# Appending each batch's new keys to its cached-key tile, a one-pass bias and a transposed head pick in a decoder step's sampled-token attention

## Chip, core and metric

The program runs on one core of one Trainium2 chip. The metric is the device time of one launch in microseconds (us). Before the change the median of three runs is 1094.81 us (1094.43 to 1094.97).

## What is computed

One inference step of a two-layer decoder on 288 tokens: 256 prompt tokens and 8 batches of 4 sampled tokens. Each layer projects the tokens, runs four mixers side by side (pooling, Conformer convolution, short convolution, sparse attention), merges them by gates, and applies a SwiGLU channel mixer and two layer norms. The part that matters here is the sampled tokens' attention: every sampled token looks at its batch's 256 cached positions (two pages of 128, found by a page table) and at its batch's up to 4 new positions, keeps the 65 best by an indexer's score, and attends to those with 8 heads of 64:

```python
ki_all = jnp.concatenate([cache_kidx.reshape(-1, IDX_DIM)[row_ids].astype(ki.dtype), ki], axis=1)
sc = index_scores(qi, ki_all, wi)
sc = jnp.where(jnp.arange(past + t)[None, None, :] <= qpos[None, :, None], sc, -jnp.inf)
vals, idx = lax.top_k(sc, ktop)
...
return sparse_attend(q, kg, vg, jnp.isfinite(vals))
```

## The kernel before

Activations stand feature by token, [128, 8, 288]. All projections go through `mm3` (L268): each float32 weight tile and each activation is split into a high and a low part of type fp32r, and three products (L271 to L273) are summed. Weights come in groups of 8 tiles (512 KB); the whole program has 306 groups, as 2448 tiles. `W` (L256) starts a turn with each group g: it issues the load of group g+5 on the SP queue, the high part of group g+3 on ACT (L245, `whi`) and the low part of group g+2 on DVE (L252, `wlo`, three buffers), and then calls `side` (L200).

`side` is the planner. Mixers and attention are generators ("tasks"). Each turn has a budget of 1.96 us of DVE and 2.3 us of ACT; the ready tasks are stepped in the order in which they were started, round after round, until one of the two budgets is used up. A task yields a pair (DVE cost, ACT cost) after what it emitted, or a number of turns to sleep, so that another engine's result is there before it goes on. All that a step emits, TensorE work too, is put on the engines' queues at that place: after the turn's `wlo` on DVE, and ahead of the group's 24 matmuls on TensorE. Tasks marked low (the convolution, 62 multiply-adds of L643 and L645 a layer) run when nothing else is ready. `finish` runs a task to its end where its result is needed.

The tasks that the change touches are two. `index_sample` (L879) loads the indexer's cached keys into one `kv` tile (16 transfers), spreads the queries into `qibd` (L886), takes scores against cached keys (L892) and, in a second bank, against all 32 new keys (L894, masked later by `vb`), sums the heads by `ws` (L902, L907), runs the top-65 on [32, 288] and leaves 0 or -1e30 per position in `sbias` (L914). `attn_sample` (L918) works on two halves f of four batches. Per half, in order:

- `load_pages("ck", f)`: eight transfers of 256 KB, each 128 partitions of 2 KB, into four `kv` tiles.
- Logits in one PSUM bank of 288 columns: the bias of each row by a float32 product with the selector `selh` (L936), four products with all new keys into columns 256 to 287 (L939), and 16 products with the cached keys, 32 rows each (L943).
- Row maximum (L948, L950 on DVE), `load_pages("cv", f)`, exponent on ACT (L954), a turn's sleep, reciprocal on DVE (L958), three transposes on TensorE (L962, L963), copies on ACT (L965, L966), a turn's sleep.
- Values: L971 for the new ones, L974 for the cached ones. Each of the 128 rows (batch, head, token) then holds 512 columns of which its own head's 64 count: DVE multiplies by the reciprocal and a head mask (L978), and TensorE picks the rows of each token with the 0/1 matrix `sel16` (L987, four float32 products of 16 columns). ACT and DVE split the result into high and low part (L992, L995).

Of the kernel before, what the change touches and what calls it, by code (L numbers as in the profile page):

```python
# [10 lines left out]
F32 = mybir.dt.float32  # L11
# [26 lines left out]
BIG = -1.0e30  # L38
# [12 lines left out]
def constants():  # L51
# [15 lines left out]
    ok = (b_[:, None] == b_[None, :]) & (t_[None, :] <= t_[:, None])  # L67
    vb = np.zeros((128, NS))
    vb[:NS] = np.where(ok, 0.0, NEG)
# [11 lines left out]
    c["selh"] = sh.reshape(128, 256)  # L81
    c["hmask"] = (h[:, None] == (np.arange(H))[None, :]) * 1.0
    c["sel16"] = ((j * TS + t)[:, None] == np.arange(16)[None, :]) * 1.0
# [10 lines left out]
    return [np.concatenate(p, 1).astype(np.float32) for p in parts], off  # L94


CONST, COFF = constants()
# [14 lines left out]
class Builder:  # L112
# [3 lines left out]
    def __init__(self, tc, ctx, d):  # L116
# [15 lines left out]
        self.hold = False  # while set, a new group's turn emits loads alone  # L132

# [97 lines left out]
    def fetch(self, g, only=0):  # L231
        """Loads, first and second parts of the groups up to so far ahead of g, or one of the three alone."""
# [74 lines left out]
    # The deviations are taken from the mean of the first half of the features, p, as soon as that is known:  # L307
    # with m the mean of d = r - p, which is at most the standard deviation, var = mean(d^2) - m^2.
    def ln_part(self, k):
        """r's chunk k is in xf (from the second half on: d's)"""  # L310
        nc, xf = self.nc, self.xf
        if k == 0:
            self.lnt = self.b([128, 4, N])
        elif k == 1:
            nc.gpsimd.tensor_tensor(self.lnt[:, 0], xf[:, 0], xf[:, 1], op=OP.add)  # L315
        elif k < 4:
            nc.gpsimd.tensor_tensor(self.lnt[:, 0], self.lnt[:, 0], xf[:, k], op=OP.add)  # L317
        else:
            self.sqs.append(k)
# [6 lines left out]
    def ln_pivot(self, scale=None):  # L326
        """xf less p, its second half scaled before"""
# [32 lines left out]
    def ln(self, g, b, after=None, fill={}):  # L360
        """fill: functions for some places that emit matrix products, and return one that takes the results away."""
# [490 lines left out]
    def load_kidx(self):  # L852
        nc, l, d = self.nc, self.l, self.d
        self.kx = self.sb.tile([128, 4, 2, 128], F32, name="kv", tag="kv", bufs=4)
        rows = slice(PHYS * l, PHYS * (l + 1))
        for b in range(NB):
            for g in range(2):
# [3 lines left out]
                nc.sync.dma_start(self.kx[64 * (b % 2):64 * (b % 2) + 64, b // 2, g],  # L861
# [4 lines left out]
    def load_pages(self, which, f):  # L866
# [3 lines left out]
        for b in range(4 * f, 4 * f + 4):  # L870
            t = self.sb.tile([128, 2, 4, 128], F32, name="kv", tag="kv", bufs=4)
            for g in range(2):
                nc.sync.dma_start(t[:, g].rearrange("p c k -> p (c k)"),
                                  d[which][rows][ds(self.page[2 * b + g], 1)].rearrange("a p k -> p (a k)"))
            out.append(t)
# [3 lines left out]
    def index_sample(self):  # L879
# [4 lines left out]
        for r in range(2):  # L884
            for h in range(4):
                nc.scalar.activation(self.qibd[64 * r:64 * r + 64, :, r, h],  # L886
                                     qv[64 * (h % 2):64 * (h % 2) + 64, h // 2, :, r], AF.Copy)
                yield 0, 0.22
        yield 1
        a, a2 = yield from self.get_ax(2)  # L890
        for p in range(4):
            nc.tensor.matmul(a[32 * p:32 * p + 32, :TP], self.qibd[:, p].rearrange("p r h t -> p (r h t)"),  # L892
                             self.kx[:, p].rearrange("p g k -> p (g k)"), start=True, stop=True)
        nc.tensor.matmul(a2[:, :NS], self.qibd.rearrange("p g r h t -> p (g r h t)"), self.ki[:, TP:],  # L894
                         start=True, stop=True)
        nc.tensor.matmul(a2[:, 64:64 + NS], self.c("hsel")[:4], self.wi[:, TP:], start=True, stop=True)
        rl = self.sb.tile([128, N], F32, name="rls", tag="rls", bufs=1)
        nc.scalar.activation(rl[:, :TP], a[:, :TP], AF.Relu, scale=0.0625)
        nc.scalar.activation(rl[:, TP:], a2[:, :NS], AF.Relu, scale=0.0625)
        yield 0, 0.6  # L900
        ws = self.sb.tile([128, NS], F32, name="ws", tag="ws", bufs=1)
        nc.vector.tensor_tensor(ws, a2[:, 64:64 + NS], self.c("delta"), op=OP.mult)  # L902
        self.free_ax(2)
# [3 lines left out]
        nc.tensor.matmul(a[:NS, :N], ws, rl, start=True, stop=True)  # L907
        sc = self.sb.tile([NS, N], F32, name="scs", tag="scs", bufs=1)
        nc.scalar.activation(sc[:, :TP], a[:NS, :TP], AF.Copy)
        nc.vector.tensor_tensor(sc[:, TP:], a[:NS, TP:N], self.c("vb")[:NS], op=OP.add)  # L910
        self.free_ax()
        yield 0.2, 0.3
        yield from self.topk(sc, NS, N, TOP_S)
        nc.vector.tensor_scalar(sc, sc, MARK, BIG, op0=OP.not_equal, op1=OP.mult)  # L914
        yield 0.3, 0
        self.sbias = sc

    def attn_sample(self):  # L918
# [12 lines left out]
        for f in range(2):  # L931
            if f:
# [3 lines left out]
            nc.tensor.matmul(a[:, :N], self.c("selh")[:NS, 128 * f:128 * (f + 1)], self.sbias,  # L936
                             start=True, stop=False)
            for c in range(4):
                nc.tensor.matmul(a[:, TP:N], self.qbd[:, c, 4 * f:4 * f + 4].rearrange("p b h t -> p (b h t)"),  # L939
                                 self.k[:, c, TP:], start=False, stop=False)  # L940
            for c in range(4):
                for j in range(4):
                    nc.tensor.matmul(a[32 * j:32 * j + 32, :TP],  # L943
                                     self.qbd[:, c, 4 * f + j].rearrange("p h t -> p (h t)"),
                                     kt[j][:, :, c], start=False, stop=c == 3)
            yield 1
            st = self.sb.tile([128, 3], F32, name="sts", tag="sts", bufs=2)
            nc.vector.tensor_reduce(st[:, 0:1], a[:, :N], axis=AX.X, op=OP.max)  # L948
# [4 lines left out]
            p = self.sb.tile([128, N], F32, name="rls", tag="rls", bufs=1)  # L953
            nc.scalar.activation(p, a[:, :N], AF.Exp, scale=0.125, bias=st[:, 0:1], accum_out=st[:, 1:2])  # L954
            self.free_ax()
            yield 0, 0.5
            yield 1
            nc.vector.reciprocal(st[:, 2:3], st[:, 1:2])  # L958
            yield 0.1, 0
# [3 lines left out]
            nc.tensor.transpose(a[:NS, 256:384], p[:, TP:], ident)  # L963
# [8 lines left out]
            for kc in range(2):  # L972
                for j in range(4):
                    nc.tensor.matmul(a[32 * j:32 * j + 32], pt[:, kc, 32 * j:32 * j + 32],  # L974
                                     vc[j][:, kc].rearrange("p c k -> p (c k)"),
                                     start=False, stop=kc == 1)
            m = yield from self.get_b([128, 512])
            nc.vector.scalar_tensor_tensor(m.rearrange("p (h d) -> p h d", h=H),  # L978
                                           a.rearrange("p (h d) -> p h d", h=H), st[:, 2:3],
                                           self.c("hmask")[:, :, None].to_broadcast([128, H, DH]),  # L980
                                           op0=OP.mult, op1=OP.mult)
            self.free_ax()
            yield 0.65, 0
            yield 1
            a = yield from self.get_ax()
            for c in range(4):
                nc.tensor.matmul(a[:, 16 * c:16 * c + 16], m[:, 128 * c:128 * (c + 1)], self.c("sel16"),  # L987
                                 start=True, stop=True)
            self.free()
            w = slice(TP + 16 * f, TP + 16 * f + 16)  # L990
            v = a[:, :64].rearrange("p (c t) -> p c t", c=4)
            nc.scalar.activation(dp[0][:, :, w], v, AF.Copy)  # L992
            yield 0, 0.25
            yield 1
            nc.vector.tensor_tensor(dp[1][:, :, w], v, dp[0][:, :, w].bitcast(F32), op=OP.subtract)  # L995
            self.free_ax()
            yield 0.15, 0
# [365 lines left out]
```

## Time and profile before

| | |
|---|---|
| median of three runs | 1094.81 us |
| profiled execution, first to last instruction | 1094.1 us |
| TensorE matmul busy | 1066.6 us (97%), 8138 instructions |
| DVE busy | 768.2 us (70%) |
| ACT busy | 557.1 us (51%) |
| GpSimd (POOL) busy | 172.0 us (16%) |
| mean granted TensorE clock | 0.995 |
| DMA | 190.24 MB, 174 GB/s on average |

The profiled execution's own time is given by its span alone, 1094.1 us; the 0.7 us between it and the median lie outside the first and last instruction or are spread between executions. TensorE's queue is in order, and so are DVE's, ACT's and SP's: an instruction that waits holds up all behind it on its engine. A float32 product is shown as two matmul instructions (x2 for one product), an fp32r product and a transpose as one. Matmuls are pipelined: a matmul's duration (0.29 us for a product of the weight stream) is longer than the distance from its start to the next one's start (0.13 us), and it is the distance that counts for TensorE's time.

### The profile page before, as it was taken

How to read it: one execution, taken by the hardware profiler on the slowest of the kernel's cores; microseconds unless marked ns; L12 is line 12 of the kernel's file. 1: busy time of each engine (PE TensorE's matmuls, PEld its weight loads, DVE VectorE, ACT ScalarE, POOL GpSimd, SP SyncE). 2: the span in 40 equal slices, each digit the busy share in tenths (PEclk: the TensorE clock that was granted, in tenths of full speed). 3: DMA queues.
4: the chain of work that ended last, by engine and by line, in shares of the span. 5: the costliest groups of instructions: out<-in, count | busy, mean ns of one | idle time of the engine just before them, and what ended most of it. 6: DMA issues, size and time to landing. Idle time of an engine off the chain costs nothing.

```text
span 1094.1 us, 20642 instructions
## 1 busy us (share of the span) xinstructions
PE 1066.6 (97%) x8138; PEld 1029.7 (94%) x8138; DVE 768.2 (70%) x1302; ACT 557.1 (51%) x928; POOL 172.0 (16%) x169
## 2 busy tenths in 40 slices
PE   8899999999999999999998999999999999999996
PEld 7889989999999999999998899899999999999995
DVE  5897868866886555544779968786587855555456
ACT  4765555454564444333576654455645644443334
POOL 0640001104410000000416300030055000000004
PEclk9999999999999999999999999999999999999998
DMA  8467557344444544554354665465443554454431
GB/s 285 158 202 266 169 206 244 130 155 166 150 159 163 173 166 156 176 171 165 137 180 144 228 242 192 143 220 191 167 160 117 183 174 164 158 174 168 171 139 44
DMA packets 60531, 190.24 MB, mean 174 GB/s; under 512 B 7026, under 2 KB 10130, under 8 KB 60434
## 3 DMA queue, kind: packets, MB, share of 16 engines
q1 hardware_dynamic: 59442, 185.35, 49.4%
q0 software_dynamic: 992, 3.57, 0.9%
q8 instruction: 64, 1.05, 0.4%
q14 instruction: 33, 0.27, 0.1%
HBM read 184.15 MB, written 4.75 MB: 173 GB/s over the span
## 4 chain that ended last, share of the span: by engine, by line
PE 84%; DVE 10%; issue 2%; POOL 2%; DMA 2%; ACT 1%; SPq 0%; DVEq 0%; POOLq 0%
PE mm L271 23%; PE mm L272 23%; PE mm L273 23%; DVE wlo L252 3%; DVE b L645 3%; PE mm L295 2%; PE mm L293 2%; PE mm L297 2%; DMA wraw<-in_w_dram 1%; PE ax L272 1%; PE ax L273 1%; PE ax L271 1%; POOL b L317 1%; POOL b L348 1%; PE ax L943 1%
## 5 line engine op out<-in xcount | busy, mean ns | idle before, releaser
L252 DVE TENSOR_TENSOR wlo<-wraw,whi 128x1024 fp32r<-128x1024 f32 (+1 forms) x307 | 382.6, 1248 | 155.6 <-issue 73.1
L273 PE MATMUL mm<-xh,wlo 128*128 128x288 f32 x1536 | 454.3, 296 | 10.8 <-DVE wlo L252 10.8
L271 PE MATMUL mm<-xh,whi 128*128 128x288 f32 x1536 | 456.3, 297 | 0.0
L272 PE MATMUL mm<-xl,whi 128*128 128x288 f32 x1536 | 453.8, 295 | 0.0
L245 ACT ACTIVATE whi<-wraw 128x1024 fp32r<-128x1024 f32 (+1 forms) x307 | 322.4, 1052 | 157.6 <-PE mm L272 80.4
L273 PEld LDWEIGHTS mm<-xh,wlo 128*128 128x128 f32 x1536 | 289.0, 188 | 13.8 <-DVE wlo L252 13.8
L271 PEld LDWEIGHTS mm<-xh,whi 128*128 128x128 f32 x1536 | 289.5, 188 | 7.8 <-issue 6.0
L272 PEld LDWEIGHTS mm<-xl,whi 128*128 128x128 f32 x1536 | 289.3, 188 | 0.4
L271 PE MATMUL mm<-b,whi 128*128 128x288 f32 x576 | 170.8, 296 | 0.4 <-DVE m L1017 0.4
L272 PE MATMUL mm<-b,whi 128*128 128x288 f32 x576 | 170.2, 295 | 0.0
L273 PE MATMUL mm<-b,wlo 128*128 128x288 f32 x576 | 169.9, 295 | 0.0
L271 PEld LDWEIGHTS mm<-b,whi 128*128 128x128 f32 x576 | 108.5, 188 | 1.3 <-DVE m L1017 0.6
L272 PEld LDWEIGHTS mm<-b,whi 128*128 128x128 f32 x576 | 108.5, 188 | 0.3
L273 PEld LDWEIGHTS mm<-b,wlo 128*128 128x128 f32 x576 | 108.4, 188 | 0.0
L1021 POOL TENSOR_TENSOR m<-m,s 128x288 f32<-128x288 f32 x32 | 36.3, 1159 | 269.1 <-DVE s L1020 269.1
L315 POOL TENSOR_TENSOR b<-xf 128x288 f32<-128x288 f32 x4 | 4.9, 1215 | 442.0 <-DVE xf L1167 433.4
L1140 ACT ACTIVATE b<-s 128x288 fp32r<-128x288 f32 x44 | 19.3, 445 | 92.1 <-DVE s L1135 92.1
L645 DVE SCALAR_TENSOR_TENSOR b<-b,prm 128x256 f32<-128x256 f32 x120 | 65.3, 600 | 0.0
L1135 DVE TENSOR_TENSOR s<-s,mm 128x288 f32<-128x288 f32 x40 | 18.0, 454 | 50.3 <-PE mm L273 50.3
L1005 ACT ACTIVATE xf<-mm 128x288 f32<-128x288 f32 x32 | 13.1, 410 | 59.3 <-PE mm L273 59.2
L1005 ACT ACTIVATE g<-mm 128x288 f32<-128x288 f32 x32 | 13.1, 410 | 58.7 <-PE mm L273 58.7
L1143 DVE TENSOR_TENSOR b<-s,b 128x288 fp32r<-128x288 f32 x44 | 19.8, 458 | 19.4 <-ACT b L1140 19.4
(252 smaller groups left out, 1230.3 us busy)
## 6 DMA issues: line engine op xcount, KB each, us to landing
wraw<-in_w_dram SPq DMA_DIRECT2D x305, 512.0 KB, 3.5
kv<-in_ck_dram SPq DMA_DIRECT2D x32, 256.0 KB, 6.0
kv<-in_cv_dram SPq DMA_DIRECT2D x32, 256.0 KB, 4.8
out_ko_dram<-b POOLq DMA_DIRECT2D x2, 576.0 KB, 4.3
out_vo_dram<-b POOLq DMA_DIRECT2D x2, 576.0 KB, 7.1
b<-in_conv_ext_dram SPq DMA_DIRECT2D x2, 558.0 KB, 5.7
kv<-in_kidx_dram SPq DMA_DIRECT2D x32, 32.0 KB, 2.8
xf<-in_x_dram SPq DMA_DIRECT2D x3, 288.0 KB, 6.6
```

The costliest lines, as they stand in the source:

```text
L245: nc.scalar.activation(t[:, c], self.raw[self.nhi][:, c], AF.Copy)
L252: nc.vector.tensor_tensor(t[:, c], raw[:, c], self.hi[self.nlo][:, c].bitcast(F32), op=OP.subtract)
L271: m(out, wh, rh, start=first, stop=False)
L272: m(out, wh, rl, start=False, stop=False)
L273: m(out, wl, rh, start=False, stop=last)
L293: m(o, wh, rh[:, k], start=k == 0, stop=False)
L295: m(o, wl, rh[:, k], start=False, stop=False)
L297: m(o, wh, rl[:, k], start=False, stop=k == nk - 1)
L645: nc.vector.scalar_tensor_tensor(o, e, wj, o, op0=OP.mult, op1=OP.add)
L1005: self.nc.scalar.activation(g, a, AF.Sigmoid)
L1021: nc.gpsimd.tensor_tensor(self.m[:, j], self.m[:, j], t, op=OP.add)
L1143: nc.vector.tensor_tensor(h[:, 1, i % 2], t, h[:, 0, i % 2].bitcast(F32), op=OP.subtract)
```

## The change

The three new or changed ideas: the four new keys of a batch are copied behind its 256 cached keys, so that one product covers 260 columns, both for the indexer and for the logits; the bias is a single fp32r product (the selector and 0 or -2^100 are exact in that type); and instead of masking heads and picking rows by products, the normalised rows are transposed, and ACT and DVE read, per 64 partitions, the columns of the right head. The new values' probabilities, now 4 columns, are spread to 32 by a DVE product with the 0/1 constant `own` before they are transposed. `selh` is loaded on its own and rounded on GpSimd; `const1` loses 292 columns.

```diff
 MARK = -3.3e38
-BIG = -1.0e30
+BIG = -(2.0 ** 100)
+NK = TP + TS
 G = 8
...
     b_, t_ = bt // TS, bt % TS
-    ok = (b_[:, None] == b_[None, :]) & (t_[None, :] <= t_[:, None])
-    vb = np.zeros((128, NS))
-    vb[:NS] = np.where(ok, 0.0, NEG)
+    vb = np.zeros((128, TS))
+    vb[:NS] = np.where(np.arange(TS)[None, :] <= t_[:, None], 0.0, NEG)
     c["vb"] = vb
...
         sh[:NS, f] = bt[:, None] == ((4 * f + j) * TS + t)[None, :]
-    c["selh"] = sh.reshape(128, 256)
-    c["hmask"] = (h[:, None] == (np.arange(H))[None, :]) * 1.0
-    c["sel16"] = ((j * TS + t)[:, None] == np.arange(16)[None, :]) * 1.0
+    selh = sh.reshape(128, 256)[:NS].astype(np.float32)
+    c["own"] = np.concatenate([((4 * f + j)[:, None] == np.arange(NB)[None, :]) * 1.0 for f in range(2)], 1)
     win = np.array([2, 4, 8, 16])
...
         nc, l, d = self.nc, self.l, self.d
-        self.kx = self.sb.tile([128, 4, 2, 128], F32, name="kv", tag="kv", bufs=4)
+        self.kx = self.sb.tile([128, 4, NK], F32, name="kv", tag="kv", bufs=4)
         rows = slice(PHYS * l, PHYS * (l + 1))
...
                     self.page[i] = nc.sync.value_load(self.pt[0:1, i:i + 1], min_val=0, max_val=PHYS - 1)
-                nc.sync.dma_start(self.kx[64 * (b % 2):64 * (b % 2) + 64, b // 2, g],
+                nc.sync.dma_start(self.kx[64 * (b % 2):64 * (b % 2) + 64, b // 2, 128 * g:128 * (g + 1)],
                                   d["kidx"][rows][ds(self.page[2 * b + g], 1)].rearrange("a p k -> p (a k)"))
...
         for b in range(4 * f, 4 * f + 4):
-            t = self.sb.tile([128, 2, 4, 128], F32, name="kv", tag="kv", bufs=4)
+            own = which == "ck"
+            t = self.sb.tile([128, 4, NK] if own else [128, 2, 512], F32, name="kv", tag="kv", bufs=4)
             for g in range(2):
-                nc.sync.dma_start(t[:, g].rearrange("p c k -> p (c k)"),
-                                  d[which][rows][ds(self.page[2 * b + g], 1)].rearrange("a p k -> p (a k)"))
+                page = d[which][rows][ds(self.page[2 * b + g], 1)]
+                if own:
+                    nc.sync.dma_start(t[:, :, 128 * g:128 * (g + 1)], page.rearrange("a p (c k) -> p (a c) k", c=4))
+                else:
+                    nc.sync.dma_start(t[:, g], page.rearrange("a p k -> p (a k)"))
+            if own:
+                nc.scalar.activation(t[:, :, TP:], self.k[:, :, TP + TS * b:TP + TS * (b + 1)], AF.Copy)
+                yield 0, 0.22
             out.append(t)
...
                 yield 0, 0.22
+        kn = self.ki[:, TP:].rearrange("p (g r t) -> p g r t", g=4, r=2)
+        for r in range(2):
+            nc.scalar.activation(self.kx[64 * r:64 * r + 64, :, TP:], kn[64 * r:64 * r + 64, :, r], AF.Copy)
+            yield 0, 0.22
         yield 1
-        a, a2 = yield from self.get_ax(2)
+        a = yield from self.get_ax()
         for p in range(4):
-            nc.tensor.matmul(a[32 * p:32 * p + 32, :TP], self.qibd[:, p].rearrange("p r h t -> p (r h t)"),
-                             self.kx[:, p].rearrange("p g k -> p (g k)"), start=True, stop=True)
-        nc.tensor.matmul(a2[:, :NS], self.qibd.rearrange("p g r h t -> p (g r h t)"), self.ki[:, TP:],
-                         start=True, stop=True)
-        nc.tensor.matmul(a2[:, 64:64 + NS], self.c("hsel")[:4], self.wi[:, TP:], start=True, stop=True)
-        rl = self.sb.tile([128, N], F32, name="rls", tag="rls", bufs=1)
-        nc.scalar.activation(rl[:, :TP], a[:, :TP], AF.Relu, scale=0.0625)
-        nc.scalar.activation(rl[:, TP:], a2[:, :NS], AF.Relu, scale=0.0625)
-        yield 0, 0.6
+            nc.tensor.matmul(a[32 * p:32 * p + 32, :NK], self.qibd[:, p].rearrange("p r h t -> p (r h t)"),
+                             self.kx[:, p], start=True, stop=True)
+        nc.tensor.matmul(a[:, 288:288 + NS], self.c("hsel")[:4], self.wi[:, TP:], start=True, stop=True)
+        rl = self.sb.tile([128, NK], F32, name="rls", tag="rls", bufs=1)
+        nc.scalar.activation(rl, a[:, :NK], AF.Relu, scale=0.0625)
+        yield 0, 0.4
         ws = self.sb.tile([128, NS], F32, name="ws", tag="ws", bufs=1)
-        nc.vector.tensor_tensor(ws, a2[:, 64:64 + NS], self.c("delta"), op=OP.mult)
-        self.free_ax(2)
+        nc.vector.tensor_tensor(ws, a[:, 288:288 + NS], self.c("delta"), op=OP.mult)
+        self.free_ax()
         yield 0.1, 0
...
         a = yield from self.get_ax()
-        nc.tensor.matmul(a[:NS, :N], ws, rl, start=True, stop=True)
-        sc = self.sb.tile([NS, N], F32, name="scs", tag="scs", bufs=1)
+        nc.tensor.matmul(a[:NS, :NK], ws, rl, start=True, stop=True)
+        sc = self.sb.tile([NS, NK], F32, name="scs", tag="scs", bufs=1)
         nc.scalar.activation(sc[:, :TP], a[:NS, :TP], AF.Copy)
-        nc.vector.tensor_tensor(sc[:, TP:], a[:NS, TP:N], self.c("vb")[:NS], op=OP.add)
+        nc.vector.tensor_tensor(sc[:, TP:], a[:NS, TP:NK], self.c("vb")[:NS], op=OP.add)
         self.free_ax()
         yield 0.2, 0.3
-        yield from self.topk(sc, NS, N, TOP_S)
-        nc.vector.tensor_scalar(sc, sc, MARK, BIG, op0=OP.not_equal, op1=OP.mult)
+        yield from self.topk(sc, NS, NK, TOP_S)
+        sbias = self.sb.tile([NS, NK], F32R, name="wi", tag="wi", bufs=1)
+        nc.vector.tensor_scalar(sbias, sc, MARK, BIG, op0=OP.not_equal, op1=OP.mult)
         yield 0.3, 0
-        self.sbias = sc
+        self.sbias = sbias
...
             a = yield from self.get_ax()
-            nc.tensor.matmul(a[:, :N], self.c("selh")[:NS, 128 * f:128 * (f + 1)], self.sbias,
-                             start=True, stop=False)
-            for c in range(4):
-                nc.tensor.matmul(a[:, TP:N], self.qbd[:, c, 4 * f:4 * f + 4].rearrange("p b h t -> p (b h t)"),
-                                 self.k[:, c, TP:], start=False, stop=False)
+            nc.tensor.matmul(a[:, :NK], self.selh[:, 128 * f:128 * (f + 1)], self.sbias, start=True, stop=False)
             for c in range(4):
                 for j in range(4):
-                    nc.tensor.matmul(a[32 * j:32 * j + 32, :TP],
+                    nc.tensor.matmul(a[32 * j:32 * j + 32, :NK],
                                      self.qbd[:, c, 4 * f + j].rearrange("p h t -> p (h t)"),
-                                     kt[j][:, :, c], start=False, stop=c == 3)
+                                     kt[j][:, c], start=False, stop=c == 3)
             yield 1
             st = self.sb.tile([128, 3], F32, name="sts", tag="sts", bufs=2)
-            nc.vector.tensor_reduce(st[:, 0:1], a[:, :N], axis=AX.X, op=OP.max)
+            nc.vector.tensor_reduce(st[:, 0:1], a[:, :NK], axis=AX.X, op=OP.max)
             yield 0.4, 0
...
             vc = yield from self.load_pages("cv", f)
-            p = self.sb.tile([128, N], F32, name="rls", tag="rls", bufs=1)
-            nc.scalar.activation(p, a[:, :N], AF.Exp, scale=0.125, bias=st[:, 0:1], accum_out=st[:, 1:2])
+            p = self.sb.tile([128, NK], F32, name="rls", tag="rls", bufs=1)
+            nc.scalar.activation(p, a[:, :NK], AF.Exp, scale=0.125, bias=st[:, 0:1], accum_out=st[:, 1:2])
             self.free_ax()
...
             yield 1
+            pn = self.sb.tile([128, NB, TS], F32, name="pn", tag="pn", bufs=1)
+            nc.vector.tensor_tensor(pn, p[:, None, TP:].to_broadcast([128, NB, TS]),
+                                    self.c("own")[:, NB * f:NB * (f + 1), None].to_broadcast([128, NB, TS]), op=OP.mult)
             nc.vector.reciprocal(st[:, 2:3], st[:, 1:2])
-            yield 0.1, 0
+            yield 0.2, 0
             a = yield from self.get_ax()
...
                 nc.tensor.transpose(a[:, 128 * kc:128 * (kc + 1)], p[:, 128 * kc:128 * (kc + 1)], ident)
-            nc.tensor.transpose(a[:NS, 256:384], p[:, TP:], ident)
+            nc.tensor.transpose(a[:NS, 256:384], pn.rearrange("p b t -> p (b t)"), ident)
             pt = self.sb.tile([128, 3, 128], F32, name="pst", tag="pst", bufs=1)
...
                 for j in range(4):
-                    nc.tensor.matmul(a[32 * j:32 * j + 32], pt[:, kc, 32 * j:32 * j + 32],
-                                     vc[j][:, kc].rearrange("p c k -> p (c k)"),
+                    nc.tensor.matmul(a[32 * j:32 * j + 32], pt[:, kc, 32 * j:32 * j + 32], vc[j][:, kc],
                                      start=False, stop=kc == 1)
             m = yield from self.get_b([128, 512])
-            nc.vector.scalar_tensor_tensor(m.rearrange("p (h d) -> p h d", h=H),
-                                           a.rearrange("p (h d) -> p h d", h=H), st[:, 2:3],
-                                           self.c("hmask")[:, :, None].to_broadcast([128, H, DH]),
-                                           op0=OP.mult, op1=OP.mult)
+            nc.scalar.activation(m, a, AF.Copy, scale=st[:, 2:3])
             self.free_ax()
-            yield 0.65, 0
+            yield 0, 0.65
             yield 1
...
             for c in range(4):
-                nc.tensor.matmul(a[:, 16 * c:16 * c + 16], m[:, 128 * c:128 * (c + 1)], self.c("sel16"),
-                                 start=True, stop=True)
+                nc.tensor.transpose(a[:, 128 * c:128 * (c + 1)], m[:, 128 * c:128 * (c + 1)], ident)
             self.free()
             w = slice(TP + 16 * f, TP + 16 * f + 16)
-            v = a[:, :64].rearrange("p (c t) -> p c t", c=4)
-            nc.scalar.activation(dp[0][:, :, w], v, AF.Copy)
-            yield 0, 0.25
+            own = []
+            for s in range(2):
+                r = slice(64 * s, 64 * s + 64)
+                e = a[r, 4 * s:]
+                e = bass.AP(tensor=e.tensor, offset=e.offset, ap=[list(e.ap[0]), [128 + 8, 4], [32, 4], [1, TS]])
+                own.append((e, *(t[r, :, w].rearrange("p c (j t) -> p c j t", j=4) for t in dp)))
+            for e, hi, lo in own:
+                nc.scalar.activation(hi, e, AF.Copy)
+                yield 0, 0.22
             yield 1
-            nc.vector.tensor_tensor(dp[1][:, :, w], v, dp[0][:, :, w].bitcast(F32), op=OP.subtract)
+            for e, hi, lo in own:
+                nc.vector.tensor_tensor(lo, e, hi.bitcast(F32), op=OP.subtract)
+                yield 0.15, 0
             self.free_ax()
-            yield 0.15, 0
         self.free(2)
...
         nc.sync.dma_start(self.cts[1], d["const1"])
+        self.selh = self.cst.tile([NS, 256], F32R, name="selh")
+        t = self.s()
+        nc.sync.dma_start(t[:NS, :256], d["selh"])
+        nc.gpsimd.tensor_copy(self.selh, t[:NS, :256])
```

## Rows read from the trace of the kernel before

**Rows 1.** The page, part 4: shares of the chain that ended last, by engine.
```profile
PE 84%; DVE 10%; issue 2%; POOL 2%; DMA 2%; ACT 1%; SPq 0%; DVEq 0%; POOLq 0%
```
**Rows 2.** Windows over both mixer stages: us, busy PE, PEld, DVE, ACT, POOL, PEclk, DMA share, GB/s.
```profile
70.00:230.00 160.00, 159.62 (x1250) 148.05 (x1249) 124.90 (x257) 82.65 (x164) 12.77 (x13) 1.00 0.59 204
611.00:780.00 169.00, 168.99 (x1321) 157.11 (x1318) 130.09 (x263) 91.51 (x172) 13.06 (x14) 1.00 0.58 201
```
**Rows 3.** Timeline of PE, layer 0, logits of f=0: start, us, engine, line.
```profile
131.17 0.30 PE L272 MATMUL mm<-xl,whi 128*128 128x288 f32 x1
131.30 0.29 PE L273 MATMUL mm<-xh,wlo 128*128 128x288 f32 x1
131.52 0.75 PE L936 MATMUL ax<-scs,const 32*128 32x288 f32 x2
132.20 1.08 PE L939 MATMUL ax<-b,qbd 128*128 128x32 f32 x8
133.21 1.93 PE L943 MATMUL ax<-kv,qbd 128*32 128x256 f32 x32
...
135.31 0.30 PE L272 MATMUL mm<-xl,whi 128*128 128x288 f32 x1
```
**Rows 4.** Chain in order of time: the row picks and four transposes of another task.
```profile
146.29 0.44 PE ax L828 x4
...
157.53 0.80 PE ax L987 x8
```
**Rows 5.** Lines by form: one transpose's own duration.
```profile
L828 PE MATMUL ax<-const,b 128*128 128x128 f32 x48 | 6.7, 273 | 0.0
```
**Rows 6.** Timeline of PE, layer 0, the indexer's products.
```profile
79.85 0.41 PE L894 MATMUL ax<-ki,qibd 128*128 128x32 f32 x2
80.18 0.41 PE L896 MATMUL ax<-wi,const 4*128 4x32 f32 x2
```
**Rows 7.** Lines by form, and one line's instructions: two prices on DVE.
```profile
L978 DVE SCALAR_TENSOR_TENSOR b<-ax,sts,const 128x512 f32<-128x512 f32 x4 | 3.0, 749 | 7.5 <-PE ax L974 7.5
L902 DVE TENSOR_TENSOR ws<-ax,const x2: 172/172/173, 83.7 to 625.4; 128x32 f32<-128x32 f32 x2
```
**Rows 8.** Timelines: the third transpose on PE and the reciprocal on DVE, all four halves.
```profile
146.78 0.27 PE L963 MATMUL ax<-const,rls 128*32 128x128 f32 x1
147.52 0.16 DVE L958 RECIPROCAL sts<-sts 128x1 f32<-128x1 f32 x1
193.87 0.27 PE L963 MATMUL ax<-const,rls 128*32 128x128 f32 x1
197.22 0.11 DVE L958 RECIPROCAL sts<-sts 128x1 f32<-128x1 f32 x1
689.91 0.27 PE L963 MATMUL ax<-const,rls 128*32 128x128 f32 x1
690.48 0.15 DVE L958 RECIPROCAL sts<-sts 128x1 f32<-128x1 f32 x1
742.60 0.27 PE L963 MATMUL ax<-const,rls 128*32 128x128 f32 x1
743.72 0.14 DVE L958 RECIPROCAL sts<-sts 128x1 f32<-128x1 f32 x1
```
**Rows 9.** Timeline of DVE, layer 0: a low part that waits for TensorE.
```profile
177.39 1.23 DVE L252 TENSOR_TENSOR wlo<-wraw,whi 128x1024 fp32r<-128x1024 f32 x1 [3.25 <-PE mm L273]
```
**Rows 10.** Windows (columns as rows 2): weight stream alone; with 512-byte indexer loads.
```profile
340.00:500.00 160.00, 160.00 (x1212) 160.00 (x1211) 88.92 (x114) 66.57 (x91) 0.00 (x0) 1.00 0.49 166
577.00:610.00 33.00, 27.51 (x200) 25.81 (x198) 32.72 (x54) 23.80 (x45) 21.98 (x20) 1.00 0.44 146
```
**Rows 11.** Layer 0, f=1: issue of the cached keys on SP, their landing, their first use.
```profile
159.45 4.16 SPq L873 DMA_DIRECT2D kv<-in_ck_dram  x8
DMA to landing us min/median/max: 4.0/4.9/5.7
171.98 1.93 PE L943 MATMUL ax<-kv,qbd 128*32 128x256 f32 x32
```

More of the change, by code (lines that the diff above doesn't have):

```diff
@@ L93, in constants @@
         parts[i].append(a)
-    return [np.concatenate(p, 1).astype(np.float32) for p in parts], off
-CONST, COFF = constants()
+    return [np.concatenate(p, 1).astype(np.float32) for p in parts], off, selh
+CONST, COFF, SELH = constants()
 PAR = {"pool_scale": (0, 2), "conv_b": (2, 2), "cg": (4, 2), "cb": (6, 2), "g1": (8, 8), "b1": (16, 8),
@@ L1255 @@
 INS = {
-    "x": (128, KD, N), "w": (NGROUPS, 128, G * 128), "const0": CONST[0].shape, "const1": CONST[1].shape, "par": (L, 128, NPAR),
+    "x": (128, KD, N), "w": (NGROUPS, 128, G * 128), "const0": CONST[0].shape, "const1": CONST[1].shape, "selh": SELH.shape, "par": (L, 128, NPAR),
     "ck": (L * PHYS, 128, 512), "cv": (L * PHYS, 128, 512), "kidx": (L * PHYS, 64, 128), "p": (L, 128, 2, N),
@@ L1301, in lay_out @@
     a["const0"], a["const1"] = CONST
+    a["selh"] = SELH
     par = np.zeros((L, 128, NPAR), f)
```

## Prediction

> **What bounds the kernel now.** I read the chain first: 84% of the path that ended last is TensorE and 10% DVE [rows 1]. Then the two stretches in which sampled attention runs, one per layer: TensorE is busy 159.6 of 160 us and 169.0 of 169 us, at a granted clock of 1.00 (2.4 GHz), with DVE at 78% and 77% and ACT at 52% and 54% [rows 2]. So there a microsecond taken off TensorE's queue is a microsecond of time, work moved between ACT and DVE is free while both keep up, and every new wait on TensorE costs its full length. Last I read the timelines around the changed products [rows 3, 4, 6, 8], because the sum needs distances between starts and not durations. A difference of under 0.2%, 2.2 us, is about what a measurement of this kernel cannot tell from no change; so the result counts as the same between 1092.6 and 1097.0.
>
> **What TensorE saves.** *Logits, four halves in all.* From the last product of the weight stream at 131.30 to the second one after the block at 135.31 are 4.01 us; two steps of the stream (131.17 to 131.30 is 0.13) would be 0.26, so the block takes 3.75 [rows 3]. Afterwards: the entry, 0.09 (131.30 to 131.52 less a step); a bias pass of fp32r with 260 columns, 0.12 (a stream step of 288 columns is 0.13); and the 16 products with their exit, 133.21 to 135.31 less one step, 1.97, which grow by 4 columns in 256 to 2.00. That is 2.21, a saving of 1.54 a half and 6.2 in all. If the bias pass gained nothing, it would keep 0.68 (131.52 to 132.20), and 3.9 would remain; below 0.12 it can't fall by more than that.
>
> *Row picks, four halves.* Four float32 products of 16 columns take 0.80; four transposes of 128 columns in another task take 0.44 [rows 4]. Saving 0.36 a half, 1.4 in all. What is given up here looks large by durations, since a transpose is shown with 273 ns [rows 5], and four would be 1.09. The Trainium skill, "TensorE: Matmul & The Clock Gate", Part 4: PE-mode transpose, puts a 128x128 transpose in one kernel's context at some 275 ns, and by that as a price for each the change would lose 1.2 us here instead. The trace agrees with the duration but not with its use as a price: the four of rows 4 start 0.11 apart. I take 0.44.
>
> *Indexer, two layers.* The product with all new keys takes 0.33 (79.85 to 80.18) [rows 6]; 0.7 in all. The cached-key and head-sum products change by 4 more and 28 fewer columns, which I leave out. Sum of savings: 6.2 + 1.4 + 0.7 = 8.3 us.
>
> **What is free.** ACT gets ten copies of new keys a layer, two 128x512 passes that DVE loses, and one extra copy a half. With the pass at DVE's 0.75 [rows 7] and each copy at no more than that, this is below 2 x 0.75 + 12 x 0.75 = 10.5 us a layer, where ACT stands idle 77 us of the stretch [rows 2]; high parts are made three turns ahead, so a copy in front of one isn't felt. Without that cover it would be felt one for one. The new pass also waits for L974, as DVE did (7.5 us of idle in the four) [rows 7]; behind it on ACT stand high parts with the same three turns of room. DVE gains: 0.75 goes, two operations of the size of L902's 0.17 come [rows 7]. At the start, `selh` adds one small load on SP ahead of `par` and the convolution state and a GpSimd copy, while `const1` shrinks by 146 KB. I take 0 for both together, between 0.4 lost (one more issue) and 0.4 gained (146 KB at 166/0.49 = 339 GB/s) [rows 10].
>
> **What the change adds to TensorE's queue: a wait.** The product with `own` is put on DVE just ahead of the reciprocal, and the third transpose, in the same turn of the planner, reads it. Before, that transpose needed only ACT's exponent of an earlier turn. Now TensorE must wait until DVE comes to this place, and DVE starts a turn late by construction: its first work of the turn is a low part, 1.2 us long, whose buffer comes free when TensorE has finished the group before; at 177.39 DVE is seen waiting 3.25 us for just that [rows 9]. So DVE can't be ahead, and side work on TensorE stands at the turn's beginning. The four reciprocals show where DVE is: they start 0.74, 3.35, 0.57 and 1.12 us after the transpose [rows 8]. Behind the transpose stands the whole weight stream.
>
> Price: the new product takes L902's 0.17 [rows 7] in the reciprocal's place, and I add as much again for the hand-over and the weight load (an estimate, by the same row). The four waits come to 1.1, 3.7, 0.9 and 1.5, 7.2 in all. The second, in layer 0, I correct. DVE runs from 177.39 without a pause to that reciprocal. The second subtraction, charged to DVE before f=1's loads, makes the planner put these loads one turn later, and with them the logits (2.2 us of TensorE), which now come after the point where DVE's run begins instead of before it, while the row maximum (0.6 with its scaling, by the planner's charges 0.5) moves into the run. So this wait falls from 3.7 to 3.7 - 2.2 + 0.6 = 2.1, and the sum to 5.6. From below, each costs the shortest seen, 0.9, so 3.6; from above, the 7.2 plus the 1.5 by which TensorE arrives earlier in a run that DVE sets, 8.7.
>
> **The cached keys' transfers.** A page now lands in runs of 512 bytes, four times as many, since a tile's row is 260 wide. The nearest row is the indexer's load, 512-byte runs too: its window moves 146 GB/s at a share of 0.44, 332 GB/s at full share, against 339 for the weights alone [rows 10]. I take the eight transfers (2.1 MB) as no slower, 6.2 us; what hides them are the turns between issue and use. In the tightest case the last lands at about 163.3 + 5.7 = 169.0, 3.0 us before its first use at 171.98 [rows 11]. On SP the next weight group is queued behind them; it is used on ACT two turns later.
>
> **Sum.** -8.3 + 5.6 = -2.7, against the profiled execution's span of 1094.1; the median of the runs is 0.7 above it, and I carry the difference to it: 1094.8 - 2.7 = 1092.1. With the bounds of the wait it is 1090.1 to 1095.2.
>
> **Rivals.** *The gain stays.* If the transposes fell into the turn after, or DVE were up with TensorE, the waits would be nil: 1094.8 - 8.3 = 1086.5. For it speaks that planner turns shift; against it that the planner's DVE charge for the new product is 0.2 of 1.96, and that all four reciprocals start after their transposes [rows 8]. Chance 0.18.
>
> *Slower: the 512-byte runs.* In the tightest half TensorE stands at L943 until the last page has landed. The burst of 6.2 us has 3.0 to spare; the time passes 1097.0 when the waits at the two f=1 halves exceed 4.9 together, for one alone when the burst takes 14.1, 2.3 times as long. If a 512-byte run cost what a 2 KB run costs now, 24.8, it would be 18.6 - 3.0 = 15.6 us there: 1107.7. Against it, the windows with 512-byte loads [rows 10]; for it, that these loads came two at a time and not eight. Chance 0.11.
>
> *It doesn't do what it says.* The bias pass stays as dear as two float32 passes: 6.2 becomes 3.9, the time 1094.4. Against it, the weight stream's step is the same type [rows 3]. Chance 0.05. *Transposes cost their duration:* 1.4 gained becomes 4 x (1.09 - 0.80) = 1.2 lost, the time 1094.7 [rows 4, 5]; against it, rows 4. Chance 0.03. This is what the Trainium skill's rule, cited above, would make of the time.
>
> **How the numbers follow.** The forecast, savings less most of a wait, has 0.63; its own range is 1090.1 to 1095.2, which the edge of 1092.6 cuts so that 0.35 lies in faster and 0.28 in same. The kept gain (0.18) is faster; dear bias and dear transposes (0.08) are the same; the 512-byte rival (0.11) is slower. Faster 0.53, same 0.36, slower 0.11. The range reaches down to the kept gain, 1086.3, and up to 1096.5, past the upper bound of the wait and the start's 0.4, and leaves out most of the 512-byte rival.
>
> **What will show it.** Right: the block of rows 3 at about 2.2 us with no L939; four transposes in 0.44 at the pick; in each half an idle TensorE in front of the third transpose, with the product by `own` on DVE named as the releaser, 1 to 2 us long; ACT's stretch share up by some points without waits of TensorE for high parts. Wrong: no such idle time (then about 1086.5), waits of TensorE at L943 for the cached keys, or the four waits over 8 us together.

## The result, and the profile after

The kernel after takes 1100.92 us (median of 4 runs, 1100.23 to 1103.24), the kernel before beside it 1094.77 (1094.43 to 1094.97). The ratio is 1.0058, with an interval of 1.0046 to 1.0071: slower by 6.1 us, where 2.7 us less were forecast, and outside the range.

What should get cheaper did. The timeline of PE in layer 1, logits of f=0 (start, us, engine, line; as rows 3):

```profile
675.01 0.29 PE L272 MATMUL mm<-xh,wlo 128*128 128x288 f32 x1
675.24 0.38 PE L944 MATMUL ax<-wi,selh 32*128 32x260 f32 x1
675.55 1.96 PE L947 MATMUL ax<-kv,qbd 128*32 128x260 f32 x32
...
677.68 0.29 PE L271 MATMUL mm<-xl,whi 128*128 128x288 f32 x1
```

Read as [rows 3] were, the block is 677.68 - 675.01 less two steps of 0.13: 2.41 us in place of 3.75. The chain shows the picks, four transposes, 0.11 apart as in [rows 4]:

```profile
155.16 0.44 PE ax L990 x4
```

That is 4 x 1.34 + 4 x 0.36 + 0.7 = 7.5 us less work on TensorE. The waits (total us, times, longest us) tell what came instead; none of these three lines is there before:

```profile
PE ax L970 <- DVE pn L963: 6.3, 4, 3.0
PE ax L947 <- DMA kv<-in_ck_dram: 2.3, 2, 1.9
PE mm L270 <- ACT whi L244: 1.0, 1, 1.0
```

The first is the forecast wait of the third transpose for the product with `own`; its four places on PE:

```profile
144.40 0.28 PE L970 MATMUL ax<-const,pn 128*32 128x128 f32 x1 [0.82 <-DVE pn L963]
196.80 0.28 PE L970 MATMUL ax<-const,pn 128*32 128x128 f32 x1 [1.85 <-DVE pn L963]
691.40 0.29 PE L970 MATMUL ax<-const,pn 128*32 128x128 f32 x1 [0.64 <-DVE pn L963]
739.54 0.29 PE L970 MATMUL ax<-const,pn 128*32 128x128 f32 x1 [2.96 <-DVE pn L963]
```

The second was listed as what would prove the forecast wrong: logits that wait for the cached keys. Timelines of SP and PE at the second half of layer 0, and the landing of its eight loads (as rows 11):

```profile
162.31 6.24 SPq L875 DMA_DIRECT2D kv<-in_ck_dram  x8
DMA to landing us min/median/max: 4.5/4.9/5.7
170.75 0.38 PE L944 MATMUL ax<-wi,selh 32*128 32x260 f32 x1
171.07 0.88 PE L947 MATMUL ax<-kv,qbd 128*32 128x260 f32 x6
173.84 3.52 PE L947 MATMUL ax<-kv,qbd 128*32 128x260 f32 x26 [1.90 <-DMA kv<-in_ck_dram]
```

From L944 to the end of L947, 170.75 to 177.36, are 6.61 us, against 675.24 to 677.51, 2.27, for the same products in the block above: 4.3 lost, of which 1.9 is named as the wait. The windows behind the two longest waits (columns as rows 2; granted clock, DMA share and GB/s last) show the rest:

```profile
172.00:174.00 2.00, 0.16 (x4) 0.19 (x8) 2.00 (x6) 0.21 (x1) 0.00 (x0) 1.00 1.01 391
174.00:176.00 2.00, 2.00 (x24) 1.23 (x17) 0.33 (x1) 0.00 (x0) 0.00 (x0) 0.50 0.93 373
176.00:178.00 2.00, 2.00 (x15) 0.92 (x8) 0.00 (x0) 0.00 (x0) 0.00 (x0) 0.65 0.11 37
...
736.00:738.00 2.00, 0.58 (x5) 0.34 (x3) 2.00 (x3) 1.36 (x2) 1.51 (x2) 1.00 0.75 248
738.00:740.00 2.00, 0.46 (x4) 0.46 (x5) 2.00 (x8) 0.13 (x1) 0.00 (x0) 1.00 0.00 0
740.00:742.00 2.00, 2.00 (x12) 2.00 (x11) 1.66 (x7) 0.40 (x2) 0.00 (x0) 0.65 0.80 262
742.00:744.00 2.00, 2.00 (x10) 2.00 (x10) 0.00 (x0) 0.00 (x0) 0.00 (x0) 0.50 0.03 8
```

TensorE stands idle for most of 172 to 174 and of 736 to 740, and then works for a while at a granted clock of 0.50 (1.2 GHz) before 1.00 (2.4 GHz) is back. Each time the windows lack 2 x 0.50 + 2 x 0.35 = 1.7 us of full clock. Before, both stretches ran at 1.00 throughout [rows 2].

The account: -7.5, +6.3 for `own`, +1.7 of clock behind its longest wait, +4.7 for the keys (4.3 with their clock in layer 0, 2.3 - 1.9 = 0.4 in layer 1), +1.0 for a high part: +6.2, against 6.1 measured.

That the two agree to 0.1 is chance; the account holds to about 1 us. A named wait counts from the modelled end of the product before it. Measured between starts, as [rows 3] were, the blocks with the waits grew by 7.0 for `own` and by 5.3 for the keys (4.4 in layer 0; 1.0 in layer 1, where only 0.4 is named):

```profile
713.03 0.29 PE L272 MATMUL mm<-xh,wlo 128*128 128x288 f32 x1
...
714.59 1.91 PE L947 MATMUL ax<-kv,qbd 128*32 128x260 f32 x26 [0.39 <-DMA kv<-in_ck_dram]
...
716.68 0.29 PE L271 MATMUL mm<-xl,whi 128*128 128x288 f32 x1
```

And the profiled execution of before has a wait for a high part at the program's start that after's does not show:

```profile
10.56 0.53 PE L293 MATMUL mm<-xh,whi 128*128 128x288 f32 x2 [1.60 <-ACT whi L245]
```

So the two spans differ by only 5.2 us, but from the first product of the weight stream on, at 28.63 before and 26.96 after, by 6.9. With the terms measured between starts the account gives +7.5.

### The profile page after: what moved, and what is told of

It is laid out like the page before. It is cut to its first block, busy times and chain, and to the rows that moved or that the text cites. A ratio compares the mean times of both kernels' runs of the same rounds, so it can differ in the third digit from the quotient of the medians.

```text
span 1099.3 us, 20570 instructions
## 1 busy us (share of the span) xinstructions
PE 1064.5 (97%) x8082; PEld 1026.3 (93%) x8082; DVE 765.1 (70%) x1306; ACT 561.4 (51%) x952; POOL 172.6 (16%) x170
## 4 chain that ended last, share of the span: by engine, by line
PE 73%; DVE 8%; issue 2%; POOL 2%; DMA 1%; ACT 1%; SPq 0%; DVEq 0%; POOLq 0%; ACTq 0%
PE mm L271 20%; PE mm L270 20%; PE mm L272 20%; DVE wlo L251 3%; DVE b L644 2%; PE mm L296 1%; PE mm L294 1%; PE mm L292 1%; DMA kv<-in_ck_dram 1%; PE ax L271 1%; PE ax L272 1%; PE ax L270 1%; POOL b L316 1%; POOL b L347 1%; PE ax L981 1%
## 5 line engine op out<-in xcount | busy, mean ns | idle before, releaser
L270 PE MATMUL mm<-xh,whi 128*128 128x288 f32 x1536 | 456.3, 297 | 1.0 <-ACT whi L244 1.0
L272 PEld LDWEIGHTS mm<-xh,wlo 128*128 128x128 f32 x1536 | 289.3, 188 | 13.7 <-DVE wlo L251 13.7
L270 PEld LDWEIGHTS mm<-xh,whi 128*128 128x128 f32 x1536 | 289.6, 189 | 9.0 <-issue 6.8
L270 PE MATMUL mm<-b,whi 128*128 128x288 f32 x576 | 170.5, 296 | 0.4 <-DVE m L1026 0.4
L270 PEld LDWEIGHTS mm<-b,whi 128*128 128x128 f32 x576 | 108.3, 188 | 1.7 <-issue 0.8
L1149 ACT ACTIVATE b<-s 128x288 fp32r<-128x288 f32 x44 | 19.3, 446 | 92.5 <-DVE s L1144 92.5
```

Of the source, the lines that this page charges most:

```text
L270: m(out, wh, rh, start=first, stop=False)
L272: m(out, wl, rh, start=False, stop=last)
L1149: nc.scalar.activation(h[:, 0, i % 2], t, AF.Copy)
```

## The experiments

The theory (A): the savings are there, and two separate things eat them, the product that DVE makes in the transpose's own turn, and cached keys that come too late; each also cost a fall of the clock. Rivals: one of the two alone is it; DVE is overfull, and any wait taken away comes back under another name; or 512-byte runs slow whatever moves.

**e1, the transposes one planner turn behind the product.**

```diff
             nc.vector.reciprocal(st[:, 2:3], st[:, 1:2])
             yield 0.2, 0
+            yield 1
             a = yield from self.get_ax()
```

> Theory A (the loss is four waits of TensorE for the product with `own`, 6 to 7 us, plus a clock that falls once behind the longest of them, some 1.7 us): with the three transposes one planner turn behind that product the waits go; idle TensorE before L971 with the product as releaser is under 1 us in all, the clock at the second half of layer 1 stays at 1.00, and the time falls by 6 to 8.5 us to 1092.5 to 1095. Rival B (the 512-byte transfers of the cached keys carry the loss, the wait only takes slack that another wait would take): the wait goes but the time falls by less than 3 us, to 1098 or more. Rival C (DVE is simply overfull around the attention, and the weight stream's low parts are late instead): the idle time moves to the wlo and whi waits and the time falls by less than 3 us.

1091.96 us, ratio to before 0.9969 (0.9958 to 0.9980): 9.0 below after, somewhat more than A gave, and far from B's and C's times. The wait for `pn` has no line left among the waits, and the clock is 1.00 in both stretches. The wait for the keys is gone too, since the half's loads and products all moved, so e1 doesn't part the two losses. And something of C is there: a wait for DVE's branch products is new, 2.76 us at 726.09. The other line below is no loss of the edit: its longest wait, 1.90, stands at 10.91, at the program's start, where before shows 1.60.

```profile
PE mm L270 <- DVE s L1030: 3.2, 2, 2.8
PE mm L292 <- ACT whi L244: 2.3, 2, 1.9
```

**e2, the keys of f=1 loaded ahead of the picks of f=0.**

```diff
-            if f:
-                kt = yield from self.load_pages("ck", f)
-                yield 1
...
             yield 0, 0.65
             yield 1
+            if f == 0:
+                kt = yield from self.load_pages("ck", 1)
             a = yield from self.get_ax()
```

> Only the second half's cached keys are loaded a planner turn earlier, ahead of the first half's row picks. Theory A: the wait for the keys at the logits of f=1 (2.3 us) goes with the clock that falls behind it (some 1.7 us in layer 0), the four waits for the product with `own` stay at 6 to 7 us: time 1096 to 1098. Rival B: keys and clock carry all the loss: 1093 to 1095. Rival D (the 512-byte runs slow whatever moves beside them): the wait shifts to the weights or to the values and the time stays at 1100 to 1102.

1094.15 us, ratio 0.9999 (0.9990 to 1.0008), 6.8 below after: more than A gave, and inside B's 1093 to 1095. The loads are issued from 151.55 for a use at 170.82, and no wait for keys is left. That is the 4.7 of the account; but the waits for `own` shrank as well, by 2.1 to a longest of 1.9, with no fall of the clock in the two stretches (1.7). Of these 8.5 us 6.8 arrived; the rest was not traced. B falls all the same, since the waits for `own` are still there and moving them takes off another 6.9 (e3):

```profile
PE ax L967 <- DVE pn L960: 4.2, 4, 1.9
```

So the two losses aren't independent: a half that starts on time meets DVE elsewhere in its turn.

**e3, both edits.**

> Both edits. Theory A: the two losses add, and what is left is the saving of TensorE's 8.3 us less at most 3 us of late high and low parts: 1086.5 to 1090. Rival C or D (another wait takes their place): 1092 or more, with the same idle time under another name.

1087.22 us (1086.79 to 1087.77), ratio 0.9931 (0.9917 to 0.9945): 7.5 below before and 13.7 below after, the fastest of all. Neither wait has a line left, and the two largest that remain are no larger than before (10.8 and 2.0 in all there):

```profile
PE mm L272 <- DVE wlo L251: 9.7, 10, 2.1
PE mm L292 <- ACT whi L244: 1.5, 1, 1.5
```

The 7.5 is the saving on TensorE as the trace of after gives it. D falls here, and C for this order of the turns: with both waits gone, no other takes their place. In other orders one does, each time for DVE's branch products: 2.8 us in e1, 1.4 in e7, 2.1 in e9 and e10. So that the whole saving survives is owed to e3's order, and not to the absence of the two waits alone.

**e4, the kernel before with 512-byte runs for the cached keys, nothing else.**

```diff
-            t = self.sb.tile([128, 2, 4, 128], ...)
+            t = self.sb.tile([128, 4, 256] if which == "ck" else [128, 2, 4, 128], ...)
...
+                    nc.sync.dma_start(t[:, :, 128 * g:128 * (g + 1)], page.rearrange("a p (c k) -> p (a c) k", c=4))
```

> The kernel before with nothing changed but the cached keys' tile, so that its loads land in 512-byte runs. Theory A: an issue of a page takes 0.57 us instead of 0.33, the last page of the second half of layer 0 lands 2 us later than before, but inside the 3.0 us that were spare: the time is 1094.5 to 1096. Rival D: the 512-byte runs alone make TensorE wait for keys or weights by 2 us or more: 1097 or above.

1094.63 us, ratio 1.0001 (0.9992 to 1.0010): as A said. Its timelines, and the durations of its issues (min, median, max ns), with those of before first:

```profile
L873 SPq DMA_DIRECT2D kv<-in_ck_dram x8: 333/333/343, 159.4 to 163.3; - x8
158.24 6.16 SPq L875 DMA_DIRECT2D kv<-in_ck_dram  x8
L875 SPq DMA_DIRECT2D kv<-in_ck_dram x8: 542/544/776, 158.2 to 163.6; - x8
DMA to landing us min/median/max: 4.3/4.5/4.7
170.77 1.93 PE L946 MATMUL ax<-kv,qbd 128*32 128x256 f32 x32
```

An issue takes 0.54 us in place of 0.33, so the burst of eight is 2.0 us longer (6.16 against 4.16); from issue to landing it takes no longer than before (4.5 against 4.9). The last page is there by 163.6 + 4.7 = 168.3, 2.5 us ahead of its use. The Trainium skill, "Perfetto Trace Analysis", What "DMA-bound" means, says that the issuing engine's slice is the making of descriptors and not the movement of data, and that large descriptors help there; the trace agrees, 0.33 against 0.54 at equal landing times.

**e5, the kernel after with 2 KB runs; the new keys enter by products of 4 columns.**

```diff
-                                     kt[j][:, c], start=False, stop=c == 3)
+                    nc.tensor.matmul(a[32 * j:32 * j + 32, :TP], q, kt[j]...[:, :, c], start=False, stop=False)
+                    nc.tensor.matmul(a[32 * j:32 * j + 32, TP:NK], q, self.k[:, c, TP + TS * b:TP + TS * (b + 1)], ...)
```

> The kernel after, but the cached keys land in 2 KB runs again, and the new keys enter by 16 products of 4 columns per half (not more than 0.12 us each, the step of a product in the block, so 0 to 7.7 us in all). Theory A1 (the transfers of 512-byte runs, two us longer in a burst, make the wait for the keys at f=1 of layer 0): the wait goes, and with it the clock's fall behind it; the block of logits grows by the new products; waits for the product with `own` stay at 4 to 7 us. Theory A2 (the wait comes from where the loads stand, a planner turn later, with their use earlier): the wait stays at 1 us or more. The time says less than the wait: 1097 to 1104.

1097.97 us, ratio 1.0025 (1.0014 to 1.0036). A1 holds: the loads stand as late as in after (issued from 162.78, used from 171.54), and no wait for keys is named. It is close: from the first product with cached keys to the stream are 2.47 us here (171.54 to 174.01) and 2.16 at f=0, so up to 0.3 of a wait may be left. The waits for `own` stay, with the fall of the clock behind the longest:

```profile
PE ax L968 <- DVE pn L961: 6.3, 4, 2.9
```

e2, e4 and e5 together are a square. From the first issue to the first use there are 12.5 us in before and in e4, 8.8 in after and in e5, 19.3 in e2; the issues take 4.2 us in before and e5, about 6 in the others. Only after has both the long issue and the short distance, and only after waits.

**e6, the kernel before with the rounded bias pass alone** (`selh` and `sbias` in fp32r, as in the diff of the change).

> The kernel before with the rounded bias pass alone. Theory A (0.12 us in place of 0.68 in each of four halves): faster by 2.2 us, 1092.5, with the product at 0.12 us. Rival (the pass costs as much as before, or what it frees is taken by another wait): 1094.3 to 1095.3.

1093.82 us, ratio 0.9991 (0.9982 to 1.0000). Faster, but not by 2.2. The timeline of PE in layer 0, f=0:

```profile
129.95 0.29 PE L273 MATMUL mm<-xh,wlo 128*128 128x288 f32 x1
130.17 0.40 PE L937 MATMUL ax<-wi,selh 32*128 32x288 f32 x1
130.50 1.08 PE L940 MATMUL ax<-b,qbd 128*128 128x32 f32 x8
```

From the pass to the next product are 0.33 us, not the stream's step of 0.13. It stands alone between products of other shapes; whether that is the reason was not tested. Against 0.68 it saves 0.35, 1.4 in all, which the interval holds.

**e7, the kernel before with the picks by transposing alone.**

> The kernel before with the heads picked by transposing alone (ACT scales and copies, DVE loses the masked pass). Theory A: four transposes in 0.44 us in place of 0.80, faster by 1.4 us, and up to 1 us more where DVE's lost pass shortens a wait: 1092.4 to 1093.4. Rival (a transpose costs its shown duration, 0.27 us): slower by 1.2 us, 1096.

1095.05 us, ratio 0.9997 (0.9988 to 1.0006): neither. The transposes are not dearer (0.44 in after's chain), but the 1.4 us don't arrive. The waits for low parts are 11.6 us against 10.8 before, which says little, as e4 has 9.6 at the time of before; a wait for DVE's branch products is new, and of the size of what is missing:

```profile
PE mm L271 <- DVE s L1023: 1.4, 1, 1.4
```

**e8, the kernel before with the wait alone**: the third transpose reads a copy of its 32 columns that DVE makes ahead of the reciprocal.

```diff
+            nc.vector.tensor_scalar(pn, p[:, TP:], 1.0, None, op0=OP.mult)
             nc.vector.reciprocal(st[:, 2:3], st[:, 1:2])
...
-            nc.tensor.transpose(a[:NS, 256:384], p[:, TP:], ident)
+            nc.tensor.transpose(a[:NS, 256:384], pn, ident)
```

> The kernel before with nothing changed but that the third transpose reads a copy that DVE makes of the new keys' weights (x 1.0, 32 columns) just ahead of the reciprocal, in the transpose's own planner turn. Theory A: four waits of TensorE for that copy, 5 to 7 us in all, slower by as much and by up to 2 us more where the clock falls behind one: 1099 to 1103. Rival (the wait takes slack that later waits for low parts would take, so it moves idle time and adds little): waits as named, but the time within 2 us of before, below 1097.

1102.88 us against 1095.46, ratio 1.0072 (1.0059 to 1.0086): as A said. The wait, and the windows of its longest one:

```profile
PE ax L965 <- DVE pn L959: 5.6, 4, 2.9
...
192.00:196.00 4.00, 1.75 (x14) 1.52 (x12) 4.00 (x6) 1.99 (x3) 2.65 (x3) 1.00 0.43 145
196.00:200.00 4.00, 3.32 (x15) 3.32 (x16) 2.81 (x12) 0.53 (x2) 0.00 (x0) 0.59 0.37 131
```

5.6 of wait and 4 x 0.41 = 1.6 of clock are 7.2 of the 7.4 us. Four operations on 32 columns, 0.13 to 0.18 us of DVE each (L959), cost by their place more than ten times what they take.

**e9, control: the kernel before with the two edits of e3.**

> Control: the kernel before with the two edits of e3 (transposes one planner turn behind the reciprocal, f=1's cached keys loaded ahead of the first half's picks) and nothing of the change. Theory A (the edits only take away what the change brought): within 1.1 us of before, 1093.7 to 1096. Rival E (the edits themselves save time, whatever the change does): 1087 to 1092.

1098.72 us, ratio 1.0028 (1.0017 to 1.0040). E falls: the edits bring nothing by themselves. A's interval is missed too: they cost 3.8, a wait for DVE's branch products in layer 1, and the clock behind it, 4 x 0.37 + 4 x 0.06 = 1.7:

```profile
PE mm L271 <- DVE s L1020: 2.1, 1, 2.1
...
724.00:728.00 4.00, 2.79 (x22) 2.55 (x20) 3.07 (x8) 3.23 (x5) 0.00 (x0) 1.00 0.97 334
728.00:732.00 4.00, 3.12 (x14) 3.15 (x15) 4.00 (x7) 0.23 (x2) 3.18 (x3) 0.63 1.01 383
732.00:736.00 4.00, 4.00 (x30) 4.00 (x30) 3.66 (x9) 2.21 (x2) 4.00 (x5) 0.94 0.41 138
```

**e10, e3 with the picks of before.**

> e3 with the row picks as before (mask on DVE, four products of 16 columns). Theory A (the picks save 4 x 0.36 us where no wait takes it): 1.4 us above e3, 1088.3 to 1089. Rival F (what the picks save is taken by waits for low parts, as in the kernel before): within 0.5 us of e3, 1086.8 to 1087.7.

1093.12 us, ratio 0.9981 (0.9972 to 0.9990), by the ratios 5.5 above e3: neither. The 1.4 of the picks are in it, and the wait of e9 is back (2.1, and a granted clock below 1.00 from 724 to 732). In e9 the row maximum (L945) and four steps of the convolution stand on DVE ahead of the branch products for which TensorE waits:

```profile
726.15 0.45 DVE L945 TENSOR_REDUCE sts<-ax 128x1 f32<-128x288 f32 x1
...
726.70 1.66 DVE L645 SCALAR_TENSOR_TENSOR b<-b,prm 128x256 f32<-128x256 f32 x4
728.28 1.54 DVE L1020 TENSOR_TENSOR s<-mm,g 128x288 f32<-128x288 f32 x4
```

In e3 the maximum comes after the first four of them. So the new picks brought nothing measurable alone (e7), and about 5 us in e3's order. Whether DVE's lost pass decides that, or the shift of turns that its charge makes, was not separated.

**e11, e3 with 2 KB runs**, as in e5.

> e3, but the cached keys land in 2 KB runs and the new keys enter by products of 4 columns. Theory A (512-byte runs cost nothing once the loads stand early enough): within 0.8 us of e3, 1086.4 to 1088. Rival D (their longer bursts still hold up weights): 1084 to 1086. Rival G (the small products cost 0.06 us or more each): 1089 or more.

1088.68 us, ratio 0.9939 (0.9926 to 0.9953): by the ratios 0.9 above e3, just over A's 0.8 and under G's 1089, and not to be told from e3, as the two intervals overlap. Once the loads stand early, 512-byte runs cost nothing that can be measured here.

## Why the prediction was wrong

- **Savings, 8.3 forecast, 7.5 found.** The picks were right to the hundredth, against the rival by which a transpose costs its duration; the block was taken as 2.21 and is 2.41. The step that failed is the bias pass, priced like a step of the weight stream [rows 3]: e6 shows 0.33 and not 0.12.
- **The free parts** held. The start can't be told from the 1.6 us by which executions differ there. ACT's extra work shows in one wait of 1.0 us at most (L270 for a high part, where the forecast's signs asked for none), which e2 has too and e3 has not.
- **The wait for `own`, 5.6 forecast, 6.3 found**; 5.6 in e8. The mechanism was right, and where DVE would be, read from the reciprocals [rows 8], was right for the first and third (1.1 and 0.9 forecast, 0.82 and 0.64 found); so was the corrected second (2.1 forecast, 1.85 found), though DVE's run behind 177.39 does have two pauses, 0.2 and 0.3 us. The fourth was 2.96 and not 1.5: its transposes came two turns of the planner earlier than before, and met DVE elsewhere. That the sum is off by only 0.7 is in part luck, three waits shorter and one twice as long.
- **The price of a wait was wrong.** The prediction took every wait at its length. The rows of before show the clock at 1.00 in these stretches [rows 2], but no wait of TensorE there is over 0.4 us; with waits of 1.9 and 3.0 us it fell twice, 3.4 us that no term held (half of it stands in the account within the keys' 4.7).
- **The cached keys, taken as no slower, were the step that failed most**, 4.7 us. Half of it was right: the moved data cost nothing, as [rows 10] suggested. But [rows 10] show bytes per time, and what grew was the time of an issue on SP, which the prediction left at 4.2 us for eight. And the 3.0 us to spare were read in the kernel before [rows 11], where from the first issue to the first use are 12.5 us. The change itself makes that 8.8: counted by the weight stream, the issue comes 42 products later and the logits only 24, which is 2.4 us, and the products for bias and new keys that stood in front of the first cached key take 1.4 us less. The slower rival named the right place (logits that stand until the last page is there), but asked for a burst 2.3 times as long; one 2 us longer did it, because the slack had shrunk.

With the corrected terms the sum is the account above, +6.2. The rival in which the gain stays gives 1086.5; e3 reaches 1087.22 with the waits taken out. (The prediction's range should have begun at that 1086.5 and not at 1086.3. Its 0.7 from span to median is another slip: in the runs behind it a launch is 1.7 to 2.1 us longer than its own span, so before's profiled execution was about 1 us slower than its median. Neither changes the outcome.)

## What to carry to other kernels

An operation that is put on one engine and read by the bounding engine in the same turn costs where the first engine stands, not what it takes; give it a turn of its own, as e1 does. Such a move shifts the turns behind it, so look through the waits for new ones, which came here in e1, e9 and e10. When a change makes the bounding engine faster, read the slack of every load again with the use moved forward, and count the issue time on the queue apart from the transfer: here it grew from 0.33 to 0.54 us with four times as many runs. Price a wait on TensorE of 2 to 3 us at its length plus a possible fall of the clock, 1.7 us here.

## What was not expected of the hardware

Every fall of TensorE's clock in the two stretches cost the same, 1.6 to 1.7 us, in after (twice), e5, e8, e9 and e10. But the length of the wait alone doesn't say whether one comes: 2.1 us idle in e9 were followed by one, 2.76 us in e1 (from 723.3 to 726.1, granted clock 1.00 in the windows on both sides) were not; and in after itself 1.90 us at 173.84 were, 1.85 us at 196.80 were not. What decides stays open. And the products of 4 columns were almost free: in e5, layer 0, f=0, from the first product with cached keys (130.05) to the first of the stream (132.21) are 2.16 us, with 16 of them between, against 1.89 (675.55 to 677.44) without: 0.02 us each.
